# A two-branch gated encoder layer in one kernel: squares over dead tiles, early embedding loads, paired output stores, a later spread of 1/rms

## The chip, the cores and the metric

The kernel runs on one core of a Trainium2 chip. The metric is the device time of one execution in microseconds (us), and the time of a version is the median of its runs. All work is in float32; the products are made of fp32r matmuls on high and low parts, so that one product of 128 x 1024 weights by 1024 x 512 activations is 24 matmuls (8 K tiles, times high by high, high by low and low by high).

## What is computed

One layer on 2048 tokens of width 1024, then a last RMSNorm. Cut to what matters here:

```python
h = _rmsnorm(x, norm_g[i])
proj = jnp.einsum('bsd,dn->bsn', h, w_in[i]) + b_in[i]
u, v, za, ab, ab_gate, zb, g_a, g_b = jnp.split(proj, SPLIT_IDX, axis=-1)
y_a = _spatial_gating_branch(gelu(u), gelu(v), za, ...)      # 128 x 128 position mixer per group
y_b = _conformer_conv_branch(ab, ab_gate, zb, ...)           # causal depthwise conv, 31 taps
merged = sigmoid(g_a) * (y_a @ w_pa[i]) + sigmoid(g_b) * (y_b @ w_pb[i])
x = x + merged @ w_out[i]
ple_gate = sigmoid(_rmsnorm(x, ple_norm_g[i]) @ w_ple_gate[i])
x = x + ple_gate * (p[i] @ w_ple[i])
return _rmsnorm(x, final_g)
```

## The kernel before

**Layout.** Activations lie transposed: 128 channels on the partitions (a K tile), tokens along the row. The tokens are two "sups" of 1024, each of two blocks of T = 512.

**Stages.** `front(sup)` norms x, makes v for 512 tokens and then for the other 512, and runs the 20 units of `ORDER` (u, z, conv and gates, seven products each, `unit`). For sup 0 the products of the per-layer embedding (`st_ple`) stand between the two halves of v; their results go to the DRAM tile `ple`. `part_a_of(sup)` multiplies branch A by w_pa. `back(sup)` multiplies branch B by w_pb (`st_pb`), the merged activations by w_out (`st_out`), and the normed result by w_ple_gate (`st_pgate`), each for block i0 and then block i1; `rms` and `x1_norm` or `finish` of one block stand beside the products of the other. The program is front(0), part_a_of(0), front(1), back(0) and part_a_of(1), back(1). The last stage of back(1) is `st_pgate` of the last block in two halves of 256 tokens (`last`), so that its first half can be finished beside the second.

**Order.** Nothing is issued by hand. `Plan` records every operation with an estimated cost and the tiles it touches, simulates PE, DVE, ACT and one queue of DMAs (SP), and pins the order of each engine to what comes out. Tiles come from rings that are opened in the order of the program (`BUFS`: 7 tiles of 512 columns in "a", 4 of 1024 in "r", 4 of 1024 in "d", 28 of 1024 in "B"). A ring's tile can be opened only when an older one is free. Each engine and the SP queue work strictly in the pinned order. So one operation that opens one tile less moves others that share its ring.

**Helpers.** Each operation is recorded in a helper, and so the profile gives most of them a helper's line: L228 two-tensor operations (`tt`), L231 scalar-tensor-tensor (`stt`), L235 `ts`, L241 ACT (`ac`; L240 a table load ahead of a logarithm), L250 matmuls, L257 DMAs. The names in the profile are rings: `a` is a work tile, `B` an activation tile or a resident weight, `s` a sum, a total of weights or an rms tile, `ps` PSUM, `r` raw weights or x.

**What the change touches.**
- `add_square` squares an updated tile of the residual into a new work tile on ACT, and DVE adds it to `b.ss`. `st_out` calls it after it adds the product to `xt` (x from DRAM), `st_pgate` after it adds the gated embedding `s * p`.
- `rms` sums `b.ss` over channels with one matmul (ps <- s, con) and makes 1/rms on ACT and DVE. For the input's norm `x_rms` does that with tiny tiles, and then spreads the factor over the partitions: four `ts` scale the identity by it into a work tile (a <- con, xs), and one float32 matmul with a matrix of constants (ps <- a, con, two records in the trace) makes `b.rx`, which `x_quarters` multiplies x by.
- `st_pgate` loads `p`, its 512 (or 256) columns of `ple`, into a work tile.
- `finish` scales one K tile of the residual and stores it.

Of the kernel before, what the change touches and what calls it, by code (L numbers as in the profile page):

```python
# [10 lines left out]
ALU = mybir.AluOpType  # L11
PSUM = bass.MemoryType.PSUM

P = 128
S = 2048
D = 1024
# [197 lines left out]
def hybrid_trunk_kernel(  # L214
# [19 lines left out]
    def ts(out, a, s0, s1, op0, op1=ALU.bypass):  # L234
        ins = nc.vector.tensor_scalar(out, a, s0, s1, op0, op1)  # L235
        plan.add("dve", out.free_size() / (0.96 if a.space == PSUM else 1.92) + 140, ins, out, a, s0, s1)
# [18 lines left out]
    def dma(out, a):  # L255
        ns = 4 * P * out.free_size() / DMA_RATE
        plan.add("dma", ns, nc.sync.dma_start(words(out), words(a)), out, a)  # L257
# [7 lines left out]
    def work(dt=F32):  # L265
        return ring("a", [T], dt)

    def slots(n, dt=F32R):

        four = [[ring("B", [2, T], dt) for _ in range(n)] for _ in range(KT // 2)]  # L270
        return [[four[k // 2][i][:, k % 2, :] for k in range(KT)] for i in range(n)]

    def psum(tag="ps", bufs=6):
        return psp.tile([P, T], F32, name=tag, tag=tag, bufs=bufs)
# [191 lines left out]
    def rsqrt_small(v, e, out, tmp):  # L466

        ac(tmp, v, AF.Ln, bias=eps[:, e : e + 1])
        ac(out, tmp, AF.Exp, scale=-0.5)
        tt(tmp, out, out, ALU.mult)  # L470
        stt(tmp, v, (RMS_EPS, LN_EPS)[e], tmp, ALU.add, ALU.mult)
        stt(out, tmp, 3.0, out, ALU.subtract, ALU.mult)
        ts(out, out, -0.5, None, ALU.mult)

    def add_square(acc, src, first, h=ALL):
        if first:
            ac(acc, src, AF.Square)
            return
        sq = work()[:, h]
        ac(sq, src, AF.Square)  # L480
        tt(acc, acc, sq, ALU.add)

# [30 lines left out]
    def x_rms(b, h):  # L513

        c = slice(h * NT, h * NT + NT)
        v, r, tmp = (b.xs[:, i, c] for i in range(3))
        ts(v, v, 1.0 / D, None, ALU.mult)
        rsqrt_small(v, 0, r, tmp)
        if h == 1:
            b.rx = ring("r", [2, T])  # L520
        ps, dg = psum(), work()
        for t in range(NT):
            ts(dg[:, t * P : (t + 1) * P], ident, r[:, t : t + 1], float(D), ALU.mult, ALU.mult)
        mm(ps, o1024, dg, True, True)
        ac(b.rx[:, h, :], ps, AF.Copy)

# [222 lines left out]
    def st_out(b, n, w, h=ALL, first=None):  # L749
        first = n == 0 if first is None else first  # L750
        xt = work()[:, h]
        dma(xt, xT[:, n, b.i * T + h.start : b.i * T + h.stop])
        if first and h.start == 0:
            (b.X,) = slots(1, F32)
            b.xnh, b.xnl = slots(2)
            b.ss, b.r = ring("s", [T]), None
        x1 = b.X[n][:, h]
        tt(x1, product(w, b.mh, b.ml, h), xt, ALU.add)
        add_square(b.ss[:, h], x1, first, h)

    def rms(b, h=ALL):
        if b.r is None:
# [7 lines left out]
        stt(t, b.X[k][:, h], half[:, 0, k : k + 1], b.r[:, h], ALU.mult, ALU.mult)  # L770
        split(b.xnh[k][:, h], b.xnl[k][:, h], t)

    def st_pgate(b, n, w, h=ALL, first=None):
        first = n == 0 if first is None else first
        p = work()[:, h]
        dma(p, ple[:, n, b.i * T + h.start : b.i * T + h.stop])
        s = work()[:, h]
        ac(s, product(w, b.xnh, b.xnl, h), AF.Sigmoid)
        x2 = b.X[n][:, h]
        tt(s, s, p, ALU.mult)  # L780
        tt(x2, x2, s, ALU.add)
        add_square(b.ss[:, h], x2, first, h)

    def finish(b, k, h=ALL):
        o = b.X[k][:, h]
        stt(o, o, half[:, 1, k : k + 1], b.r[:, h], ALU.mult, ALU.mult)
        dma(outT[:, k, b.i * T + h.start : b.i * T + h.stop], o)


    blocks = [Block(i) for i in range(NB)]  # L790
# [3 lines left out]
    def do(f, *a):  # L794
        seq.append((0.0, None, lambda w: f(*a)))

    def std(w, n, f, *a):
        seq.append((5.5, lambda: load_w(w, n), lambda got: f(*a, got)))
# [15 lines left out]
    def ple_of(i, c, w):  # L814
        if w:
            ple_w[c] = w
        st_ple(i, c, ple_w[c])
# [3 lines left out]
    def front(b, first, then):  # L821
        def G(j):
            two(b, 32, j, st_gate)
            two(b, 24, j, st_ab)

        def A(j):
            two(b, 0, j, st_u)
            two(b, 16, j, st_za)

        def zb(j):  # L830
            two(b, 40, j, st_keep, AF.Silu, 40, "zb")

        def ga(j):
            two(b, 48, j, st_keep, AF.Sigmoid, 48, "ga")

        def gb(j):
            two(b, 56, j, st_keep, AF.Sigmoid, 56, "gb")

        square = [(x_square, b, t) for t in range(2 * NT)]
        rms = [(x_rms, b, h) for h in range(2)]  # L840
        quarters = [(x_quarters, b, k) for k in range(4)]
        if first:
            beside = [square[4:6], square[6:], rms[1:], [], square[:2], square[2:4], rms[:1] + [(p_split, 0)], [(p_split, 1)]]
            for j, v in enumerate(v_items(b, 1)):
                if j < 4:
                    do(x_raw, b, j)
                if j == 1:
                    do(load_constants)
                std(*v)
                for e in beside[j]:  # L850
                    do(*e)
            do(load_more_constants)
            for j in range(2 * NB):
                i, c = divmod(j, 2)
                seq.append((5.5, (lambda c=c: load_w(w_ple, c)) if i == 0 else None, lambda got, i=i, c=c: ple_of(i, c, got)))
                if c:
                    do(*quarters[i])
                    if i + 2 < NB:
                        do(p_split, i + 2)
            for j in range(8):  # L860
                seq.append((5.5, lambda j=j: load_w(w_v, j, True), lambda got, j=j: st_v(b, 0, j, got)))
            do(setup_mixer)
        else:
            for j, v in enumerate(v_items(b, 1)):
                std(*v)
                if j >= 4:
                    do(*quarters[j - 4])
            mix(v_items(b, 0), [])
        do(v_rms, b)
        if not first:  # L870
            do(pace, 3)
        for f, j in ORDER:
            if (f, j) == ORDER[-1]:
                do(*then)
            dict(G=G, A=A, z=zb, a=ga, b=gb)[f](j)

    def part_a_of(s, rest):
        both = blocks[2 * s : 2 * s + 2]
        for j in range(KT):
            us = 11.0  # L880
            seq.append((us, lambda j=j: load_w(w_pa, j), lambda got, j=j: [st_pa(i, j, got) for i in both]))
            for r in rest[j * len(rest) // KT : (j + 1) * len(rest) // KT]:
                do(*r)

    def back(s, then):
        i0, i1 = blocks[2 * s], blocks[2 * s + 1]
        for n in range(KT):
            std(w_pb, n, st_pb, i0, n)
            if n == 4:
                do(y_load, i1, "yb")  # L890
        for n in range(KT):
            std(w_pb, n, st_pb, i1, n)
        for n in range(KT):
            std(w_out, n, st_out, i0, n)
        mix([(w_out, n, st_out, i1, n) for n in range(KT)], [(rms, i0)] + [(x1_norm, i0, k) for k in range(KT)])
        mix([(w_pg, n, st_pgate, i0, n) for n in range(KT)], [(rms, i1)] + [(x1_norm, i1, k) for k in range(KT)])
        rest = [(rms, i0)] + [(finish, i0, k) for k in range(KT)]
        if then:
            mix([(w_pg, n, st_pgate, i1, n) for n in range(KT)], rest[:5] + then[:1] + rest[5:] + then[1:])
            return [(rms, i1)] + [(finish, i1, k) for k in range(KT)]  # L900
        held = {}

        def last(n, h):
            def run(w):
                held[n] = w or held[n]
                st_pgate(i1, n, held[n], h)

            return run

        halves = [slice(0, T // 2), slice(T // 2, T)]  # L910
        for n in range(KT):
            seq.append((2.9, lambda n=n: load_w(w_pg, n, stay=n < 6), last(n, halves[0])))
            if n == 1:
                do(rms, i0)
        rest = [(finish, i0, k) for k in range(KT)]
        rest[4:4] = [(rms, i1, halves[0])]
        for n in range(KT):
            seq.append((2.9, None, last(n, halves[1])))
            for r in rest[n * len(rest) // KT : (n + 1) * len(rest) // KT]:
                do(*r)  # L920
        do(rms, i1, halves[1])
        for h in halves:
            for k in range(KT):
                do(finish, i1, k, h)
# [11 lines left out]
    b = sups[1]  # L936
    early = [(x_square, b, t) for t in (4, 5, 6, 7)] + [(x_rms, b, 1)] + [(x_raw, b, k) for k in range(4)]
    do(pace, 1)
    part_a_of(0, early + [(x_square, b, t) for t in range(4)] + [(x_rms, b, 0)])
    do(pace, 2)  # L940
    front(sups[1], False, (y_load, blocks[0], "yb"))
    do(pace, 4)
# [79 lines left out]
```

## Time and profile before

| | us |
|---|---|
| median of 3 runs | 2138.9 (2136.34 to 2139.3) |
| the profiled execution, its own time | 2135.81 |
| its span (first to last instruction) | 2133.9 |
| PE busy (TensorE matmuls) | 2089.7, 98% |
| DVE busy (VectorE) | 1672.6, 78% |
| ACT busy (ScalarE) | 1070.4, 50% |
| mean granted TensorE clock | 0.990 of 2.4 GHz |

The span is what the trace covers; the execution's own time is 1.9 us longer, and the median of the runs another 3.1 us. Busy times are sums over the span. In a timeline, consecutive instructions of one kind are put into one row: start, length from the first to the last one's end, engine, line, operation, and the count, and in brackets the engine's idle time before the row and what ended it. PE rows of one product or many are 24 matmuls or a multiple, unless another kind stands between them.

### The profile page before, as it was taken

To read this page: it belongs to the slowest core of one execution; us is meant where nothing else is said; L and a number is where in the kernel's file an instruction comes from. 1 tells how busy PE (TensorE), PEld (TensorE's weight loads), DVE (VectorE), ACT (ScalarE), POOL (GpSimd) and SP (SyncE) were. 2 spreads that over 40 slices of the span, in tenths; PEclk is the share of its full clock that TensorE was granted. 3 is DMA by queue.
4 is the path that set the end of the run, shared out by engine and by line. 5 is a ranking of instruction groups with operands and counts; after the bars stand their busy time and mean duration, and the time that the engine had idled before them with its cause. 6 is when DMAs were issued, how large, how long until landed. Compare 5 with 4: busy or idle time off the path is not lost.

```text
span 2133.9 us, 26416 instructions
## 1 busy us (share of the span) xinstructions
PE 2089.7 (98%) x9354; PEld 1717.3 (80%) x9354; DVE 1672.6 (78%) x2237; ACT 1070.4 (50%) x1542; POOL 0.2 (0%) x4
## 2 busy tenths in 40 slices
PE   9999999999999999999999999999999999999997
PEld 7878888888888878878878788887888877888877
DVE  4777999999999969878879898889866774464675
ACT  6635464555556733255445555556544551232453
POOL 0000000000000000000000000000000000000000
PEclk9999999999999999999999999999999999999999
DMA  8888878788688877787677687778744466674433
GB/s 292 300 335 324 289 260 319 264 313 309 264 321 319 287 276 251 252 278 261 207 257 227 223 293 242 245 257 270 255 152 139 148 233 204 206 236 134 146 121 109
DMA packets 205156, 523.73 MB, mean 245 GB/s; under 512 B 22368, under 2 KB 43232, under 8 KB 205024
## 3 DMA queue, kind: packets, MB, share of 16 engines
q1 hardware_dynamic: 205024, 522.05, 71.1%
q8 instruction: 73, 1.20, 0.2%
q14 instruction: 59, 0.48, 0.1%
HBM read 326.81 MB, written 195.16 MB: 245 GB/s over the span
## 4 chain that ended last, share of the span: by engine, by line
PE 89%; DMA 4%; DVE 3%; ACT 2%; issue 1%; SPq 0%; DVEq 0%; ACTq 0%
PE ps L250 88%; PE pq L250 1%; DMA r<-w_v 1%; DMA r<-x 1%; DVE d L231 1%; ACT a L241 1%; DMA a<-ple 1%; DVE B L228 1%; DVE a L228 0%; DMA w<-w 0%; DVE w L228 0%; ACT w L241 0%; ACT d L241 0%; DMA r<-V 0%; DVE a L231 0%
## 5 line engine op out<-in xcount | busy, mean ns | idle before, releaser
L250 PE MATMUL ps<-B,w 128*128 128x512 f32 (+1 forms) x7680 | 1773.0, 390 | 13.4 <-ACT B L241 4.5
L250 PEld LDWEIGHTS ps<-B,w 128*128 128x128 f32 x7680 | 1434.8, 188 | 328.2 <-ACT a L241 12.1
L231 DVE SCALAR_TENSOR_TENSOR d<-c,cw,d 128x1024 f32<-128x1024 f32 x464 | 574.2, 1281 | 3.3 <-ACT d L241 2.9
L228 DVE TENSOR_TENSOR w<-r,w 128x1024 fp32r<-128x1024 f32 (+1 forms) x208 | 209.6, 1008 | 158.1 <-PE ps L250 109.2
L241 ACT CAST w<-r 128x1024 fp32r<-128x1024 f32 (+1 forms) x208 | 182.0, 876 | 273.7 <-PE ps L250 226.9
L228 DVE TENSOR_TENSOR a<-ps,a 128x512 f32<-128x512 f32 x176 | 121.3, 689 | 92.8 <-PE ps L250 60.0
L250 PE MATMUL ps<-w,B 128*128 128x512 f32 x768 | 183.1, 399 | 6.2 <-ACT B L241 2.8
L250 PEld LDWEIGHTS ps<-w,B 128*128 128x128 f32 x768 | 146.7, 192 | 42.1 <-ACT w L241 4.3
L241 ACT COPY a<-ps 128x512 f32<-128x512 f32 x88 | 51.0, 590 | 186.4 <-PE ps L250 185.9
L241 ACT ACT_TABLE_LOAD x93 | 119.3, 1283 | 2.3 <-PEq L1013 0.7
L241 ACT CAST B<-a 128x512 fp32r<-128x512 f32 x128 | 76.4, 619 | 70.0 <-DVE a L228 38.7
L228 DVE TENSOR_TENSOR a<-a 128x512 f32<-128x512 f32 (+1 forms) x136 | 86.6, 657 | 30.5 <-ACT a L241 20.9
L241 ACT ACTIVATE a<-ps,bi 128x512 f32<-128x512 f32 x96 | 66.2, 689 | 81.7 <-PE ps L250 81.2
L228 DVE TENSOR_TENSOR B<-a,B 128x512 fp32r<-128x512 f32 x128 | 84.7, 689 | 27.4 <-ACT B L241 27.2
L241 ACT CAST w<-s 128x512 fp32r<-128x512 f32 x112 | 69.0, 618 | 66.2 <-issue 30.0
L228 DVE TENSOR_TENSOR n<-d,n 128x512 fp32r<-128x512 f32 (+1 forms) x96 | 65.9, 688 | 21.4 <-ACT d L241 10.3
L228 DVE TENSOR_TENSOR w<-s,w 128x512 fp32r<-128x512 f32 x112 | 76.6, 688 | 5.6 <-ACT w L241 5.1
L241 ACT ACTIVATE a<-a,bi 128x512 f32<-128x512 f32 x96 | 68.8, 720 | 23.1 <-DVE a L228 22.2
L241 ACT ACTIVATE a<-B 128x512 f32<-128x512 f32 (+1 forms) x63 | 36.8, 584 | 71.3 <-DVE B L228 71.3
L241 ACT ACTIVATE a<-ps 128x512 f32<-128x512 f32 (+1 forms) x96 | 53.4, 557 | 36.0 <-PE ps L250 35.9
L240 ACT ACT_TABLE_LOAD x47 | 60.3, 1283 | 0.8
L241 ACT CAST B<-r 128x512 fp32r<-128x512 f32 (+1 forms) x62 | 39.6, 664 | 37.5 <-DVE r L231 23.5
(79 smaller groups left out, 1169.6 us busy)
## 6 DMA issues: line engine op xcount, KB each, us to landing
w<-w SPq DMA_DIRECT2D x392, 512.0 KB, 4.1
r<-w_s SPq DMA_DIRECT2D x56, 512.0 KB, 5.4
r<-w_pb SPq DMA_DIRECT2D x32, 512.0 KB, 4.3
r<-w_out SPq DMA_DIRECT2D x32, 512.0 KB, 3.5
r<-w_pg SPq DMA_DIRECT2D x32, 512.0 KB, 3.5
a<-xT SPq DMA_DIRECT2D x48, 256.0 KB, 3.9
c<-glu SPq DMA_DIRECT2D x16, 527.0 KB, 5.2
r<-w_v SPq DMA_DIRECT2D x16, 512.0 KB, 5.9
```

Source lines behind the costliest of these rows:

```text
L228: plan.add("dve", out.free_size() / 0.96 + 152, nc.vector.tensor_tensor(out, a, b, op), out, a, b)
L231: ins = nc.vector.scalar_tensor_tensor(out, a, s, b, op0, op1)
L240: load = [nc.scalar.preload_act_table_set("natural_log_exp_and_others")] if both else []
L241: ins = nc.scalar.copy(out, a) if func == AF.Copy and not kw else nc.scalar.activation(out, a, func, **kw)
L250: plan.add("pe", ns, pe.matmul(out, lhsT=lhsT, rhs=rhs, start=start, stop=stop, **kw), out, lhsT, rhs)
```

## The change

1. `add_square` gets the tile to write the square over: `xt` in `st_out`, `s` in `st_pgate`. It opens no work tile.
2. In the last block's `st_pgate`, `p` of two K tiles and all 512 columns is one DMA of 512 KB into a tile of ring "d", and serves both halves: 4 DMAs in the place of 16 of 128 KB. The `rms` of block i0 is traced after the third half product and not after the second.
3. `finish` stores at every second K tile, two K tiles in one DMA: 20 stores in the place of 40.
4. The spread of 1/rms is a function of its own, `x_spread`, and is traced later than `x_rms`.

```diff
+    class Tiles(list):
+        pass
+
     def slots(n, dt=F32R):
 
         four = [[ring("B", [2, T], dt) for _ in range(n)] for _ in range(KT // 2)]
-        return [[four[k // 2][i][:, k % 2, :] for k in range(KT)] for i in range(n)]
+        out = []
+        for i in range(n):
+            out.append(Tiles(four[k // 2][i][:, k % 2, :] for k in range(KT)))
+            out[i].tiles = [f[i] for f in four]
+        return out
...
-    def add_square(acc, src, first, h=ALL):
+    def add_square(acc, src, first, sq):
         if first:
             ac(acc, src, AF.Square)
             return
-        sq = work()[:, h]
         ac(sq, src, AF.Square)
         tt(acc, acc, sq, ALU.add)
...
         rsqrt_small(v, 0, r, tmp)
+
+    def x_spread(b, h):
+
         if h == 1:
             b.rx = ring("r", [2, T])
         ps, dg = psum(), work()
         for t in range(NT):
-            ts(dg[:, t * P : (t + 1) * P], ident, r[:, t : t + 1], float(D), ALU.mult, ALU.mult)
+            r = b.xs[:, 1, h * NT + t : h * NT + t + 1]
+            ts(dg[:, t * P : (t + 1) * P], ident, r, float(D), ALU.mult, ALU.mult)
...
-        add_square(b.ss[:, h], x1, first, h)
+        add_square(b.ss[:, h], x1, first, xt)
...
-    def st_pgate(b, n, w, h=ALL, first=None):
-        first = n == 0 if first is None else first
-        p = work()[:, h]
-        dma(p, ple[:, n, b.i * T + h.start : b.i * T + h.stop])
+    def st_pgate(b, n, w, h=ALL, p=None):
+        first = n == 0
+        if p is None:
+            p = work()
+            dma(p, ple[:, n, b.tok])
...
-        add_square(b.ss[:, h], x2, first, h)
+        add_square(b.ss[:, h], x2, first, s)
...
-        dma(outT[:, k, b.i * T + h.start : b.i * T + h.stop], o)
+        if k % 2:
+            dma(outT[:, k - 1 : k + 1, b.i * T + h.start : b.i * T + h.stop], b.X.tiles[k // 2][:, :, h])
...
-            beside = [square[4:6], square[6:], rms[1:], [], square[:2], square[2:4], rms[:1] + [(p_split, 0)], [(p_split, 1)]]
+            beside = [square[4:6], square[6:], rms[1:], [], square[:2] + spread[1:], square[2:4], rms[:1] + [(p_split, 0)], [(p_split, 1)]]
...
+                if j == 0:
+                    do(*spread[0])
...
             for j, v in enumerate(v_items(b, 1)):
                 std(*v)
+                if j == 0:
+                    do(*spread[0])
...
-                st_pgate(i1, n, held[n], h)
+                if n % 2 == 0 and w:
+                    held["p"] = ring("d", [2, T])
+                    dma(held["p"], ple[:, n : n + 2, i1.tok])
+                p = held.setdefault((n, "p"), held["p"][:, n % 2, :])
+                st_pgate(i1, n, held[n], h, p[:, h])
...
-            if n == 1:
+            if n == 2:
                 do(rms, i0)
...
-    part_a_of(0, early + [(x_square, b, t) for t in range(4)] + [(x_rms, b, 0)])
+    part_a_of(0, early + [(x_square, b, t) for t in range(4)] + [(x_rms, b, 0), (x_spread, b, 1)])
```

Where the planner puts things differs in four places only: the first 60 us, the end of part_a_of(0) with the start of front(1), the end of back(0), and back(1). Three of them follow.

On PE at the start of the program: `ps<-w,B` are v products (sup 0, the second 512 tokens), `ps<-d,w` the products of the embedding, `ps<-a,con` the two spreads.

```order
-L250 MATMUL ps<-w,B 128x512 x73
-L250 MATMUL ps<-a,con 128x512
-L250 MATMUL ps<-w,B 128x512 x111
-L250 MATMUL ps<-a,con 128x512
-L250 MATMUL ps<-w,B 128x512 x8
-L250 MATMUL ps<-d,w 128x512 x192
+L250 MATMUL ps<-w,B 128x512 x132
+L250 MATMUL ps<-a,con 128x512
+L250 MATMUL ps<-w,B 128x512 x60
+L250 MATMUL ps<-d,w 128x512 x24
+L250 MATMUL ps<-a,con 128x512
+L250 MATMUL ps<-d,w 128x512 x168
```

Both spreads moved back, the second of them from 8 matmuls ahead of the embedding's products to 24 matmuls into them. In front(1) they moved too: before, the first stood 240 matmuls ahead of the end of part_a_of(0) and the second at that end; now the first stands at that end, and the second one v product (24 matmuls) later.

On the SP queue at the end of back(0), before (`ya_117` is branch A's result in DRAM, `outT` the output, `ple` the embedding's products, `w_pa` weights of the next stage):

```order
L257 DMA r<-w_pa 128x1024
L257 DMA outT<-B 128x512 x3
L257 DMA a<-ya_117 128x512 x8
L257 DMA a<-ple 128x512
L257 DMA r<-w_pa 128x1024 x3
L257 DMA a<-ple 128x512
L257 DMA a<-ya_117 128x512 x8
L257 DMA a<-ple 128x512
```

The same place in the changed kernel:

```order
L257 DMA r<-w_pa 128x1024
L257 DMA outT<-B 128x2x512
L257 DMA a<-ya_117 128x512 x6
L257 DMA outT<-B 128x2x512
L257 DMA a<-ya_117 128x512 x2
L257 DMA a<-ple 128x512 x2
L257 DMA r<-w_pa 128x1024 x2
L257 DMA a<-ya_117 128x512 x4
L257 DMA outT<-B 128x2x512
L257 DMA a<-ya_117 128x512 x4
L257 DMA a<-ple 128x512
```

Two `a<-ple` moved ahead of the weights of the next stage, and between the two groups of eight `a<-ya_117` stand two loads of weights and not three.

On the SP queue through the last two stages of back(1) (`w_pg` weights of `st_pgate`), before:

```order
L257 DMA r<-w_pg 128x1024 x2
L257 DMA a<-ple 128x512
L257 DMA r<-w_pg 128x1024
L257 DMA a<-ple 128x512
L257 DMA r<-w_pg 128x1024
L257 DMA a<-ple 128x256 x4
L257 DMA outT<-B 128x512
L257 DMA a<-ple 128x256
L257 DMA outT<-B 128x512 x5
L257 DMA a<-ple 128x256
L257 DMA outT<-B 128x512 x2
L257 DMA a<-ple 128x256 x9
```

And in the changed kernel, to the end of the queue:

```order
L257 DMA r<-w_pg 128x1024
L257 DMA a<-ple 128x512
L257 DMA r<-w_pg 128x1024
L257 DMA a<-ple 128x512
L257 DMA r<-w_pg 128x1024 x2
L257 DMA a<-ple 128x512
L257 DMA r<-w_pg 128x1024
L257 DMA outT<-B 128x2x512 x4
L257 DMA outT<-B 128x2x256 x8
```

The loads of 256 columns are gone from here (the four loads in their place stand earlier, among the weights of the w_pb stage of back(1)), and only output stores are left behind the last weights.

## Rows read from the trace of the kernel before

**Rows 1.** The page: busy time, share of the span and instructions of each engine.

```profile
PE 2089.7 (98%) x9354; PEld 1717.3 (80%) x9354; DVE 1672.6 (78%) x2237; ACT 1070.4 (50%) x1542; POOL 0.2 (0%) x4
```

**Rows 2.** Waits of PE over the whole span: us in total, times, longest.

```profile
PE ps L250 <- ACT B L241: 10.5, 4, 4.5
PE ps L250 <- DVE s L228: 7.8, 3, 4.6
```

**Rows 3.** Windows: length, busy us (instructions) of the engines, PEclk, DMA share, GB/s.

```profile
750.00:775.00 25.00, 22.83 (x92) 18.11 (x91) 16.18 (x23) 11.51 (x17) 0.00 (x0) 0.93 0.89 311
1750.00:1775.00 25.00, 19.13 (x69) 14.33 (x68) 16.76 (x25) 11.19 (x18) 0.00 (x0) 0.86 0.77 257
2050.00:2100.00 50.00, 44.96 (x292) 41.09 (x290) 38.54 (x64) 24.59 (x42) 0.00 (x0) 0.93 0.40 136
```

**Rows 4.** Timeline of PE, then DVE, at the start of front(1).

```profile
753.48 1.13 PE L250 MATMUL ps<-a,con 128*128 128x512 f32 x2 [2.17 <-DVE a L235]
...
810.92 87.62 PE L250 MATMUL ps<-w,B 128*128 128x512 f32 x384
...
867.58 0.68 DVE L228 TENSOR_TENSOR B<-r,B 128x512 fp32r<-128x512 f32 x1
```

**Rows 5.** Timeline of SP, DVE, ACT and PE at the end of back(0).

```profile
1741.30 8.05 SPq L257 DMA_DIRECT2D r<-w_pa  x3
...
1749.91 7.19 SPq L257 DMA_DIRECT2D a<-ya  x8
...
1753.29 0.69 DVE L228 TENSOR_TENSOR a<-a 128x512 f32<-128x512 f32 x1 [2.25 <-DMA a<-ple]
...
1754.80 0.63 ACT L241 ACTIVATE a<-B 128x512 f32<-128x512 f32 x1 [4.00 <-DVE B L228]
...
1755.99 8.50 PE L250 MATMUL ps<-B,w 128*128 128x512 f32 x24 [4.46 <-ACT B L241]
1765.87 1.13 PE L250 MATMUL ps<-s,con 128*128 128x512 f32 x2 [1.38 <-DVE s L228]
```

**Rows 6.** Timeline of SP, ACT and PE as the last stage of back(1) begins.

```profile
2057.91 2.07 SPq L257 DMA_DIRECT2D r<-w_pg  x2
2060.03 0.43 SPq L257 DMA_DIRECT2D a<-ple  x1
...
2066.95 0.63 ACT L241 ACTIVATE a<-B 128x512 f32<-128x512 f32 x1 [4.92 <-DVE B L228]
...
2068.63 4.87 PE L250 MATMUL ps<-B 128*128 128x256 f32 x24 [3.23 <-ACT B L241]
2075.26 1.86 PE L250 MATMUL ps<-s,con 128*128 128x512 f32 x2 [1.76 <-DVE s L228]
```

**Rows 7.** Timeline of ACT, DVE and PE in the last 16 us.

```profile
2119.11 0.37 ACT L241 ACTIVATE a<-ps 128x256 f32<-128x256 f32 x1
...
2121.14 0.42 DVE L228 TENSOR_TENSOR a<-a 128x256 f32<-128x256 f32 x1
...
2123.32 1.22 PE L250 MATMUL ps<-s,con 128*128 128x256 f32 x2 [4.63 <-DVE s L228]
...
2127.26 3.26 DVE L231 SCALAR_TENSOR_TENSOR B<-B,half,s 128x256 f32<-128x256 f32 x8
```

**Rows 8.** Timeline of DVE, SP and ACT as the embedding's products begin.

```profile
53.50 0.88 DVE L235 TENSOR_SCALAR a<-con,xs 128x128 f32<-128x128 f32 x4
...
60.03 1.39 SPq L257 DMA_DIRECT2D V<-a  x3
...
66.55 1.09 ACT L241 COPY a<-ps 128x512 f32<-128x512 f32 x2 [0.40 <-DMA V<-a]
```

**Rows 9.** DMA issues: count, KB each, median us from issue to landing.

```profile
V<-a SPq DMA_DIRECT2D x32, 256.0 KB, 3.8
...
outT<-B SPq DMA_DIRECT2D x24, 256.0 KB, 3.2
...
outT<-B SPq DMA_DIRECT2D x16, 128.0 KB, 1.8
```

More of the change, by code (lines that the diff above doesn't have):

```diff
@@ L839, in front @@
         square = [(x_square, b, t) for t in range(2 * NT)]
-        rms = [(x_rms, b, h) for h in range(2)]
+        rms, spread = ([(f, b, h) for h in range(2)] for f in (x_rms, x_spread))
         quarters = [(x_quarters, b, k) for k in range(4)]
         if first:
-            beside = [square[4:6], square[6:], rms[1:], [], square[:2], square[2:4], rms[:1] + [(p_split, 0)], [(p_split, 1)]]
+            beside = [square[4:6], square[6:], rms[1:], [], square[:2] + spread[1:], square[2:4], rms[:1] + [(p_split, 0)], [(p_split, 1)]]
             for j, v in enumerate(v_items(b, 1)):
```

## The prediction

> **What bounds the kernel now.** I read the page's busy times first: TensorE works for 2089.7 of 2133.9 us, 98% [rows 1]. So nothing that runs beside it counts, and what can be won is in its gaps and in the stretches at half clock. Next PE's waits by releaser: the two largest entries are a cast on ACT (ACT B, four gaps, 10.5 us) and the sum of squares on DVE (DVE s, three gaps, 7.8 us) [rows 2]. Then the windows around these gaps, which give idle time and clock together [rows 3]: a 25 us window loses 25 less PE's busy time, and (1 − clock) x 25 more. In 750 to 775 us that is 2.17 + 1.75 = 3.9 us; in 1750 to 1775, 5.87 + 3.5 = 9.4; in the 50 us from 2050, 5.04 + 3.5 = 8.5. Last the timelines of the engines at these places [rows 4 to 8], to see what each gap waits for. The change moves work in just these places and at the start.
>
> **Second front (751 us).** Before, the first spread's matmul stands between products of part_a, and PE waits 2.17 us for its four scalings on DVE [rows 4]. Now it stands behind all of them, 240 matmuls later; a matmul takes 87.62/384 = 0.228 us [rows 4], so DVE has some 55 us more. The second spread stands one product (24 x 0.228 = 5.5 us) later than it did, which starts the four quarters of x later; their last DVE step was at 867.58 and they are needed when the v products end, at 810.92 + 87.62 = 898.5 [rows 4]. Those 30 us of slack hide it. I take the whole loss, **−3.9**; with the gap alone and no clock it is −2.2.
>
> **End of back(0) (1751 us).** SP stands in three loads of w_pa for 8.05 us [rows 5], and one `a<-ple` and eight `a<-ya` queue behind them. DVE then idles 2.25 us for that `a<-ple`; its add releases the square, which ACT waited 4.00 us for; behind the square in ACT's order are the casts of branch A's tiles, and PE, at 1755.99, has waited 4.46 us for one of them. DVE is then late with the sum of squares too: another 1.38 us of PE [rows 5]. Now two `a<-ple` go ahead of the weights, eight `a<-ya` ahead of both, and the square opens no tile of ring "a", so loads into it are let go sooner. The casts can pass ACT before the late squares. What is late next would be the last eight `a<-ya`, behind two w_pa loads in place of three: by 8.05 x 2/3 = 5.4 us of SP they are 2.7 us sooner, and the last `a<-ple` is no longer ahead of them. I take nearly all of the 9.4: **−9.3**; the gaps alone (4.46 + 1.38) are −5.8.
>
> **Last stage (2065 us).** Again `a<-ple` is issued behind two loads (w_pg, 2.07 us of SP), ACT waits 4.92 us for the add and PE 3.23 us for the cast behind the square, then 1.76 us for the sum of squares [rows 6]. Now a load of w_pg and one of ple alternate, no loads of half tiles crowd ring "a", and `rms` comes one half product later. PE has two half products of 24 matmuls to work on ahead of it and not one; 24 took 4.87 us at the lower clock [rows 6] and would take about 2.9 at the full one (an estimate: 4.87 with 1.75 to 2 us of clock loss taken off). The sum must follow its product by an eviction, two adds, a square and an add, so I leave 0.6 us of waiting: 8.5 − 0.6 = **−7.9**; the gaps alone are −5.0, and nothing left to wait −8.5.
>
> **Tail.** After the last product PE idles 4.63 us for the sum [rows 7]. In it the gate is evicted by 2119.48, but DVE takes it at 2121.14, since scalings of the first half stand ahead of it. With `rms` of the first half one product sooner in DVE's new order, most of these 1.66 us go; I take 1.3. Against that, the last stores are of 256 KB: a store of that size lands in 3.2 us, one of 128 KB in 1.8 [rows 9], so +1.4, less one issue at the end, which takes 1.39/3 = 0.46 us [rows 8]. Together −1.3 + 1.4 − 0.5 = **−0.4**, between −2.0 (landing no longer, and all 1.66) and +0.9 (DVE no sooner).
> The Trainium skill, "DMA: Bandwidth & Descriptors", Anatomy of one DMA, gives each transfer a fixed part and bytes at 436 GB/s; by that 128 KB more cost 0.3 us, an estimate, and the tail would be −1.5. Its fit is of another way of issuing; the sum here goes by the rows.
>
> **Start.** Here the change adds a wait. The second spread's four scalings took 0.88 us and were in time [rows 8]; now its matmul stands 24 matmuls into the embedding's products, and its work tile comes free only when a store of v has landed. Three such stores are issued from 60.03 us, a store takes 3.8 us by its median [rows 9], and ACT, waiting for one of them, went on only at 66.55 [rows 8], 6.5 us after. So the scalings start between 63.8 and 66.5 and end 0.9 us later, while PE is there at about 63 (the embedding's products began at some 58, and 24 matmuls are 5.5). PE waits 1.7 to 4.4 us, in order, with all later products queued behind it, and may lose 1.75 us of clock as it did after the gap at 753 [rows 3]. I take 2.2 + 1.75, less 0.6 for small waits for the embedding's inputs, which are now loaded sooner: **+3.3**. The ends are −0.6 (the store lands in time) and +6.7 (4.4 + 1.75, and 0.6 at the first spread, which is now 59 matmuls later). The quarters start later here as well; as above, what they feed is far off.
>
> Squares over dead tiles and early ple loads cost nothing themselves: the same squares, and four loads of 512 KB in a stage where the DMA engines are busy 0.40 of the time or so [rows 3].
>
> **Sum:** −3.9 − 9.3 − 7.9 − 0.4 + 3.3 = −18.2, against the profiled execution's 2135.8: 2117.6. The runs' median stands 3.1 above that execution, so **2120.7** for the median. The ends: −3.9 − 9.4 − 8.5 − 2.0 − 0.6 = −24.4 (2114.5), and with gaps alone −2.2 − 5.8 − 5.0 + 0.9 + 6.7 = −5.4 (2133.5).
>
> **The rivals.**
> *Start clean.* The store lands in time and the early wait is −0.6: 2120.7 − 3.9 = 2116.8. The median of 3.8 speaks for it, the 6.5 of just that place against.
> *The stall at 1751 comes back.* Two loads of w_pa still hold SP ahead of the last `a<-ya`, and if the casts of the second eight wait as long as the first did, 9.3 us are not won: 2130.0.
> *The clock stays.* Behind each gap the rows show a half-clock stretch [rows 3], and I took them for its effect. If they are not, 1.75 + 3.5 + 3.5 us stay and the start loses none: 2120.7 + 8.75 − 1.75 = 2127.7. [...]
> *No change.* With PE at 98%, each wait just moves to the next late cast: 2138.9. The slack in rows 4 speaks against it.
> *Slower.* A tile that holds x or the gate now lives on through the square and the sum. If the seven tiles of ring "a" then come free later, the next product's eviction waits for a tile, PSUM stays full and PE waits: at the DVE wait of 2.25 us [rows 5] in each of the 16 products of the two `st_pgate` stages that stand beside loads of other tiles, 36 us, 2156.7. It makes the kernel slower from (18.2 + 4.3)/16 = 1.4 us in each. Against it: a product opens two tiles now and not three, and lasts 5.5 us, so a tile would have to live for some 19 us.
>
> **How the numbers follow.** A measurement of this kernel tells 0.2%, 4.3 us, from no change. Forecast 0.55, start clean 0.12, stall back 0.14, clock 0.06: all faster, 0.87. No change 0.07. Slower 0.06. The range takes in the four faster cases and most of the bounds: 2113 to 2132.
>
> **What would show it.** Right: no PE wait on DVE a near 751, none over 1 us on ACT B near 1751 and 2065, clock 1.00 in these windows, a new wait of 1 to 4 us for DVE a near 63 us, and about 3.3 us for the last sum. Wrong: `a<-ya` casts still late behind w_pa, or a gap of PE in front(1) ahead of its first unit. The rest of the trace should be as before, shifted.

## The result, and the profile after

The changed kernel takes 2114.64 us (median of 4 runs, 2111.93 to 2115.85), the kernel before 2137.62 in the same runs (2133.91 to 2139.3). The ratio is 0.990, 95% interval 0.9881 to 0.9918. That is 23.0 us less, where 18.2 were forecast; the forecast time was 2120.7 with a range of 2113 to 2132. The profiled execution took 2111.93 us, its span is 2109.3 and its mean granted clock 0.995. Ratios are of the fast runs alone: two executions beside the experiments, of 4254.91 and 8261.13 us, are left out of them.

The page's span and busy times:

```profile
span 2109.3 us, 26318 instructions
...
PE 2077.8 (99%) x9354; PEld 1709.7 (81%) x9354; DVE 1670.5 (79%) x2237; ACT 1071.1 (51%) x1542; POOL 0.2 (0%) x4
```

PE's busy time fell by 11.9 us, from 2089.7 to 2077.8 [rows 1], with the same 9354 matmuls. Nearly all of that is clock: the granted mean rose from 0.990 to 0.995, some 11 us over the span (an estimate). The other half of the span's 24.6 us, 12.7 us, is gaps.

PE's waits by releaser (us in total, times, longest):

```profile
PE ps L250 <- ACT w L241: 4.0, 2, 3.3
PE ps L250 <- DMA w<-w: 4.0, 2, 2.3
PE ps L250 <- DVE s L228: 3.8, 2, 2.6
...
PE ps L250 <- ACT B L241: 1.9, 1, 1.9
PE ps L250 <- DVE a L235: 1.5, 1, 1.5
```

ACT B went from 10.5 us to 1.9, and that one wait is in the first 8 us; DVE s from 7.8 to 3.8 [rows 2]. The wait for the spread's scalings, DVE a L235, is still there, but at another place (61 us). What leads now, casts of w_v and loads of kept weights, was there before, with 2.8 and 4.3 us.

The windows that answer to [rows 3]: length, busy us (instructions) of PE, PEld, DVE, ACT and POOL, PEclk, DMA share, GB/s. The places have moved up by 0 to 21 us.

```profile
740.00:765.00 25.00, 24.34 (x108) 19.80 (x107) 21.74 (x30) 17.89 (x26) 0.00 (x0) 1.00 0.85 300
1745.00:1770.00 25.00, 23.79 (x103) 19.03 (x102) 19.09 (x27) 10.72 (x15) 0.00 (x0) 1.00 0.89 307
2045.00:2095.00 50.00, 50.00 (x393) 48.65 (x392) 37.34 (x72) 26.29 (x50) 0.00 (x0) 1.00 0.25 88
```

Clock 1.00 in all three, against 0.93, 0.86 and 0.93; idle 0.7, 1.2 and 0 us, against 2.2, 5.9 and 5.0.

To see where the time goes, I compare when PE reaches the same work in the two profiles. In the kernel before (timeline of PE: start, length, operation, idle time ahead and its releaser), besides the row of the sum at 1765.87 [rows 5] and that of the last sum at 2123.32 [rows 7]:

```profile
743.39 0.40 PE L250 MATMUL pq<-n,conr 128*128 128x512 f32 x1
...
898.37 6.96 PE L250 MATMUL ps<-B,w 128*128 128x512 f32 x30
...
1200.69 5.53 PE L250 MATMUL ps<-B,w 128*128 128x512 f32 x16 [2.26 <-DMA w<-w]
...
2112.77 5.92 PE L250 MATMUL ps<-B,w 128*128 128x256 f32 x48
```

In the changed kernel:

```profile
743.40 0.40 PE L250 MATMUL pq<-n,conr 128*128 128x512 f32 x1
...
894.49 5.83 PE L250 MATMUL ps<-B,w 128*128 128x512 f32 x25
...
1195.21 10.97 PE L250 MATMUL ps<-B,w 128*128 128x512 f32 x40 [2.32 <-DMA w<-w]
...
1753.20 1.12 PE L250 MATMUL ps<-s,con 128*128 128x512 f32 x2 [1.21 <-DVE s L228]
...
2091.30 5.92 PE L250 MATMUL ps<-B,w 128*128 128x256 f32 x48
2099.79 0.75 PE L250 MATMUL ps<-s,con 128*128 128x256 f32 x2 [2.57 <-DVE s L228]
```

| from, to | forecast | what PE gained there |
|---|---|---|
| start to the conv's matmul at 743 us | +3.3 | 743.40 − 743.39 = 0.0 |
| to the first unit of front(1) | −3.9 | 894.49 − 898.37 = −3.9 |
| to a wait for kept weights near 1200 us | 0 | −5.5, so −1.6 |
| to the sum of squares at the end of back(0) | −9.3 | 1753.20 − 1765.87 = −12.7, so −7.2 |
| to the last two products | −7.9 | 2091.30 − 2112.77 = −21.5, so −8.8 |
| to the end | −0.4 | spans 2109.3 − 2133.9 = −24.6, so −3.1 |
| sum | −18.2 | −24.6 |

The three large terms came about, one to the tenth, one 2.1 us smaller and one 0.9 us larger than forecast. The rest of the difference is in the start, in a stretch that the change does not touch, and in the tail.

SP at the end of back(0), against [rows 5]:

```profile
1733.90 2.30 SPq L257 DMA_DIRECT2D r<-w_pa  x2
1736.30 2.21 SPq L257 DMA_DIRECT2D a<-ya  x4
...
1740.04 4.52 SPq L257 DMA_DIRECT2D a<-ya  x4
```

The last eight `a<-ya` are issued from 1736.30 in two groups, and not from 1749.91. SP still stands 2.3 us in w_pa loads, but no longer 8.05.

### The profile page after: what moved, and what is told of

It is laid out like the page before. It is cut to its first block, busy times and chain, and to the rows that moved or that the text cites. A ratio compares the mean times of both kernels' runs of the same rounds, so it can differ in the third digit from the quotient of the medians.

```text
span 2109.3 us, 26318 instructions
## 1 busy us (share of the span) xinstructions
PE 2077.8 (99%) x9354; PEld 1709.7 (81%) x9354; DVE 1670.5 (79%) x2237; ACT 1071.1 (51%) x1542; POOL 0.2 (0%) x4
## 4 chain that ended last, share of the span: by engine, by line
PE 90%; DMA 5%; DVE 3%; ACT 2%; issue 1%; SPq 0%; DVEq 0%; ACTq 0%
PE ps L250 88%; PE pq L250 1%; DMA a<-ya 1%; DMA r<-w_v 1%; DVE d L231 1%; ACT a L241 1%; DMA r<-w_ple 0%; DVE w L228 0%; DVE B L228 0%; DMA w<-w 0%; ACT w L241 0%; ACT d L241 0%; DVE a L228 0%; DMA r<-V 0%; SPq L257 0%
## 5 line engine op out<-in xcount | busy, mean ns | idle before, releaser
L228 DVE TENSOR_TENSOR a<-a 128x512 f32<-128x512 f32 x120 | 79.7, 685 | 9.8 <-ACT a L241 8.7
L228 DVE TENSOR_TENSOR s<-s,a 128x512 f32<-128x512 f32 (+1 forms) x63 | 39.6, 629 | 27.0 <-ACT a L241 26.8
```

The lines of the kernel that those rows point to most:

```text
L228: plan.add("dve", out.free_size() / 0.96 + 152, nc.vector.tensor_tensor(out, a, b, op), out, a, b)
```

## The experiments

Two theories were set against each other for the large terms. Theory one: a square in a work tile of its own takes one of seven slots of ring "a", and with it the order in which loads are let go. Theory two: the 32 DMAs fewer (12 embedding loads and 20 stores; the first expectation counts 36) relieve the SP queue. Ratios are to the kernel before in runs made beside each experiment; the changed kernel's own is 0.990 (0.9881 to 0.9918).

**Squares in ring a again.**

```diff
-        ac(sq, src, AF.Square)
+        sq = work()[:, : src.free_size()]
+        ac(sq, src, AF.Square)
```

> The changed kernel with squares written into a new work tile again; all else as changed. Theory one (a square's tile costs a slot of the seven in ring a, and so sets the order in which the SP queue lets loads go): the order of the end of back(0) and of the last w_pg loads goes most of the way back, PE waits some 3 to 4.5 us for a cast near 1750 us and 2 to 3 us as the last stage begins, each with half clock behind it: +9 to +14 us, 2124 to 2129. Theory two (early loads of ple and paired stores, 36 DMAs fewer, relieve the SP queue): those stay, so within 2 us of the changed kernel, about 2115.

Measured: 2127.59 us, ratio 0.9972 (0.9959 to 0.9985). Its timeline of PE at the two places, and of SP at the first:

```profile
1757.63 8.93 PE L250 MATMUL ps<-B,w 128*128 128x512 f32 x24 [4.71 <-ACT B L241]
1767.95 1.13 PE L250 MATMUL ps<-s,con 128*128 128x512 f32 x2 [1.38 <-DVE s L228]
...
2071.09 6.22 PE L250 MATMUL ps<-B 128*128 128x256 f32 x36 [2.16 <-ACT B L241]
...
1750.30 0.33 SPq L257 DMA_DIRECT2D r<-w_pa  x1
1750.73 0.37 SPq L257 DMA_DIRECT2D a<-ple  x1
1751.20 7.55 SPq L257 DMA_DIRECT2D a<-ya  x8
```

The waits of before are back (4.71 and 1.38 us where 4.46 and 1.38 stood, and 2.16 in the last stage where 3.23 stood), and the last eight `a<-ya` are issued from 1751.20, as late as before. All other parts of the change were in this kernel. Theory two is out as the cause of these waits. By the medians this kernel is still 7.0 us faster than the one before: no wait stands near 751 us, the sum in the last stage waits 0.41 us in place of 1.76, and the last sum 3.43 in place of 4.63.

**Squares in ring n.** Is it the slot in "a", or the shorter chain when a tile is overwritten?

```diff
-        ac(sq, src, AF.Square)
+        sq = ring("n", [T])[:, : src.free_size()]
+        ac(sq, src, AF.Square)
```

> The changed kernel with squares in a tile of their own again, but of ring n, which is free in these stages, and not of ring a. Theory one (only the slot in ring a counts): the gains at 1750 us and in the last stage stay, PE's waits there below 1.3 us, within 3 us of the changed kernel: 2112 to 2116. Rival (writing over the dead tile itself brings the gain, by a shorter chain from add to square to sum): back to the kernel with squares in ring a, 2125 to 2130.

Measured: 2116.07 us, ratio 0.9912 (0.9893 to 0.9932). PE, then SP, at the end of back(0):

```profile
1734.71 20.79 PE L250 MATMUL ps<-B,w 128*128 128x512 f32 x91
1757.10 1.12 PE L250 MATMUL ps<-s,con 128*128 128x512 f32 x2 [1.60 <-DVE s L228]
...
1737.99 5.47 SPq L257 DMA_DIRECT2D a<-ya  x7
```

No wait for a cast, 1.60 us for the sum, which is a little over the 1.3 expected, and none in the last stage; seven of the last eight `a<-ya` are issued from 1737.99, early as in the changed kernel. The square may have a tile of its own, but not one of this ring: it is the slot.

**Squares over dead tiles alone**, on the kernel before:

```diff
-    def add_square(acc, src, first, h=ALL):
+    def add_square(acc, src, first, sq):
...
-        sq = work()[:, h]
...
-        add_square(b.ss[:, h], x1, first, h)
+        add_square(b.ss[:, h], x1, first, xt)
...
-        add_square(b.ss[:, h], x2, first, h)
+        add_square(b.ss[:, h], x2, first, s)
```

> The kernel before with the first part of the change alone: squares over the dead tiles. Theory: this part alone takes the gap near 1750 us down to 0.5 to 1.5 us and that at the last stage's beginning down as well, where the second sum (rms of block 2 after the second half product) still waits 1.5 to 2.5 us; the gap of 2.2 us at 751 us stays. Against the kernel before -10 to -14 us, 2121 to 2126. Rival: it needs the early loads of ple too, so that ring a is free in the last stage; then the last stage keeps its waits of 3.2 and 1.8 us and only some 7 us are won, 2128 to 2130.

Measured: 2121.29 us against 2133.06, ratio 0.9942 (0.9926 to 0.9957): −11.8 us of medians, about half of the whole gain. Its timeline of PE:

```profile
751.15 1.12 PE L250 MATMUL ps<-a,con 128*128 128x512 f32 x2 [2.17 <-DVE a L235]
...
1739.67 18.07 PE L250 MATMUL ps<-B,w 128*128 128x512 f32 x79
1757.97 1.13 PE L250 MATMUL ps<-s,con 128*128 128x512 f32 x2 [0.23 <-DVE s L228]
...
2062.77 1.13 PE L250 MATMUL ps<-s,con 128*128 128x512 f32 x2 [2.39 <-DVE s L228]
```

At the end of back(0) 0.23 us are left; in the last stage only the wait for the second sum, 2.39; the wait of 2.17 us at 751 us stays, as it should. This kernel has as many loads and stores as the one before, so the waits for the casts go without fewer DMAs. The wait ahead of the last sum goes down too, to 2.63 us from 4.63.

**The last block's embedding loaded late again** (16 DMAs of 128 KB into ring "a"):

```diff
-                if n % 2 == 0 and w:
-                    held["p"] = ring("d", [2, T])
-                    dma(held["p"], ple[:, n : n + 2, i1.tok])
-                p = held.setdefault((n, "p"), held["p"][:, n % 2, :])
-                st_pgate(i1, n, held[n], h, p[:, h])
+                p = work()[:, h]
+                dma(p, ple[:, n, i1.i * T + h.start : i1.i * T + h.stop])
+                st_pgate(i1, n, held[n], h, p)
```

> The changed kernel with the last block's ple loaded per half and per K tile again (16 DMAs of 128 KB into ring a). Theory one: the last stage still begins without a wait, because loads of ple for block 2 still alternate with w_pg; the end loses 0 to 2 us by adds that wait for late ple tiles: 2115 to 2117. Theory two: the wait as the last stage begins comes back with its clock, +5 to +8: 2120 to 2123.

Measured: 2114.33 us, ratio 0.9906 (0.9886 to 0.9926): its interval covers no difference from the changed kernel. Its trace has no wait of PE over 0.4 us in the last stage, and 2.63 us ahead of the last sum (2.57 with the early loads). With the squares out of ring "a", the loads of half tiles crowd nothing.

**The sum one half product sooner:**

```diff
-            if n == 2:
+            if n == 1:
                 do(rms, i0)
```

> The changed kernel with rms of block 2 traced after the second half product again. Theory: the sum of squares is not ready when PE comes to it one half product (2.9 us) sooner: a wait of 0.5 to 3 us for DVE s near 2055 us, +0.5 to +4.5 with clock: 2115 to 2119. Rival: the loads come so much sooner that the sum is ready anyway: no wait, 2114 to 2115.

Measured: 2116.45 us, ratio 0.9919 (0.9898 to 0.994). PE in the last stage:

```profile
2065.17 2.07 PE L250 MATMUL ps<-s,con 128*128 128x512 f32 x2 [2.39 <-DVE s L228]
```

The wait comes back, 2.39 us, and the two records of the sum take 2.07 us where the same two take 1.13 at full clock (in the kernel with squares over dead tiles alone): half clock stands behind it in this profile (granted clock 0.76 from 2062 to 2068 us). The median of the runs is only 1.8 us above that of the changed kernel and its interval covers no difference, so the wait is shown and its price is not. Of the last stage's gain it is a part that the squares do not bring.

**Single stores again:**

```diff
-        if k % 2:
-            dma(outT[:, k - 1 : k + 1, b.i * T + h.start : b.i * T + h.stop], b.X.tiles[k // 2][:, :, h])
+        dma(outT[:, k, b.i * T + h.start : b.i * T + h.stop], o)
```

> The changed kernel with one store for each K tile again (40 stores). By the landing times of the rows (256 KB 3.2 us, 128 KB 1.8) the end after the last scaling would be 1.4 us shorter less 0.5 for the issues: -0.9. Rival (what ends the kernel is the number of issues and the fixed part of a transfer): the same or up to 1 us longer. At 1750 us PE's waits as in the changed kernel. In all 2113 to 2117.

Measured: 2118.14 us, ratio 0.9919 (0.9901 to 0.9937), 1 us above what was expected, and not told apart from the changed kernel by its interval. In its profile the last scaling ends at 2114.28 and the span at 2118.0, 3.7 us later; in the changed kernel these are 2106.17 and 2109.3, 3.1 us. In the other two profiles with single stores, the kernel before and the one with squares over dead tiles alone, it is 3.4 and 3.3 us. So pairing shortens the very end by 0.2 to 0.6 us; the forecast had it 0.9 longer.

**The second front's spreads, back at the sums.**

```diff
-    part_a_of(0, early + [(x_square, b, t) for t in range(4)] + [(x_rms, b, 0), (x_spread, b, 1)])
+    part_a_of(0, early + [(x_square, b, t) for t in range(4)] + [(x_rms, b, 0), (x_spread, b, 0)])
...
-    early = [(x_square, b, t) for t in (4, 5, 6, 7)] + [(x_rms, b, 1)] + [(x_raw, b, k) for k in range(4)]
+    early = [(x_square, b, t) for t in (4, 5, 6, 7)] + [(x_rms, b, 1), (x_spread, b, 1)] + [(x_raw, b, k) for k in range(4)]
...
                 std(*v)
-                if j == 0:
-                    do(*spread[0])
```

> The changed kernel with the second front's two spreads traced where they were before (directly behind their sums of squares). If the wait of 2.17 us at 751 us and its half clock were the spread's place alone: +3 to +4 us, 2118 to 2118.5, all of it between 740 and 760 us. If that time had only moved to the waits at 742, 913 and 1393 us that the changed kernel has: no difference, 2114 to 2115.

Measured: 2109.9 us, ratio 0.9896 (0.9875 to 0.9917): not slower. But its DVE and PE near 751 us show that this was not a true undo:

```profile
744.50 0.87 DVE L235 TENSOR_SCALAR a<-con,xs 128x128 f32<-128x128 f32 x4
...
751.03 1.02 PE L250 MATMUL ps<-a,con 128*128 128x512 f32 x2
```

The first spread stands on PE where it stood before, with no wait, because DVE's four scalings are done by 745.4. Two more items beside part_a's products than before had shifted the planner's order on DVE. So I undid it exactly, with the spread inside `x_rms` for the second sup:

```diff
         rsqrt_small(v, 0, r, tmp)
+        if b.s:
+            x_spread(b, h)
...
-    part_a_of(0, early + [(x_square, b, t) for t in range(4)] + [(x_rms, b, 0), (x_spread, b, 1)])
+    part_a_of(0, early + [(x_square, b, t) for t in range(4)] + [(x_rms, b, 0)])
...
                 std(*v)
-                if j == 0:
-                    do(*spread[0])
```

> The changed kernel with the second front's spreads inside x_rms again, so that part_a_of(0) has the same 14 items beside its products as before (the earlier undo had 16, which shifted them); on PE and DVE the order around 751 us is that of the kernel before. Theory: the gap of about 2 us for DVE a returns at 751 us, with or without 1.7 us of half clock behind it: +2 to +4 in the stretch 740 to 765 us. Rival (the gap was never the spread's place, but DVE being late for other reasons): no gap there, as in the earlier undo.

Measured: 2118.7 us, ratio 0.9921 (0.9903 to 0.9939). DVE and PE:

```profile
754.07 0.67 DVE L235 TENSOR_SCALAR a<-con,xs 128x128 f32<-128x128 f32 x3
...
754.79 2.00 PE L250 MATMUL ps<-a,con 128*128 128x512 f32 x2 [2.17 <-DVE a L235]
```

The gap of 2.17 us is back to the hundredth, and the two records take 2.00 us where they took 1.02 above: half clock again (granted clock 0.86 from 750 to 762 us). The median is 4.1 us above that of the changed kernel, but the intervals overlap: the gap is shown by the profile, its price in the runs is not. Tracing the spread later is enough to be rid of it, but not needed: the matmul may stay if the scalings do not stand behind the conv's taps on DVE.

**The first front's spreads, back at the sums:**

```diff
-            beside = [square[4:6], square[6:], rms[1:], [], square[:2] + spread[1:], square[2:4], rms[:1] + [(p_split, 0)], [(p_split, 1)]]
+            beside = [square[4:6], square[6:], rms[1:] + spread[1:], [], square[:2], square[2:4], rms[:1] + spread[:1] + [(p_split, 0)], [(p_split, 1)]]
...
-                if j == 0:
-                    do(*spread[0])
                 if c:
```

> The changed kernel with the first front's two spreads traced where they were before. Theory: the wait of 1.3 to 2.4 us for DVE a near 61 us, which all profiles of the late spread show, goes, and 0.6 us of small waits for inputs of the embedding's products come back: -0.7 to -1.8 us, 2112.5 to 2115. Rival: the later stores of v and loads of p cost as much: the same or 1 us slower, up to 2117.

Measured: 2116.16 us, ratio 0.9923 (0.9908 to 0.9937). No wait near 61 us, but 2.8 us near 28 and 1.4 near 56 us, ahead of the spreads' matmuls at their old places: no gain, as the rival had it.

**Only the second of them moved back:**

```diff
-            beside = [square[4:6], square[6:], rms[1:], [], square[:2] + spread[1:], square[2:4], rms[:1] + [(p_split, 0)], [(p_split, 1)]]
+            beside = [square[4:6], square[6:], rms[1:], [], square[:2] + spread[1:], square[2:4], rms[:1] + spread[:1] + [(p_split, 0)], [(p_split, 1)]]
...
-                if j == 0:
-                    do(*spread[0])
                 if c:
```

> The changed kernel with only the second spread of the first front moved back to its sum of squares; the first stays at its late place. Theory: the wait near 61 us goes while the inputs of the embedding's products are still loaded early: -1.3 to -2.4 us, 2112 to 2114. Rival: the time comes back at the waits for casts of w_v near 113 to 126 us: no difference, 2114 to 2117.

Measured: 2112.91 us, ratio 0.9906 (0.9887 to 0.9924). The wait is 0.69 us; the interval covers no difference.

**rx in ring d for the first sup**, to free ring "r" for the weights of v:

```diff
         if h == 1:
-            b.rx = ring("r", [2, T])
+            b.rx = ring("r" if b.s else "d", [2, T])
```

> The changed kernel with the first sup's rx (the spread 1/rms) in ring d and not in r, a version that could beat both. Theory: PE's waits near 112 and 118 us for casts of w_v (0.7 and 3.3 us, and half clock behind) come from ring r, where rx holds one of four tiles while x quarters hold two; with it gone w_v is loaded sooner: -4 to -7 us, 2107.5 to 2110.5. Rival: the loads of w_v are late because the SP queue has the stores of ple ahead of them, which PE's own pace sets: no difference, 2114 to 2115.

Measured: 2116.32 us, ratio 0.9921 (0.9898 to 0.9945). PE in the first front:

```profile
65.42 1.80 PE L250 MATMUL ps<-a,con 128*128 128x512 f32 x2 [3.66 <-DVE a L235]
...
123.94 3.24 PE L250 MATMUL ps<-w,B 128*128 128x512 f32 x12 [0.75 <-ACT w L241]
127.90 19.35 PE L250 MATMUL ps<-w,B 128*128 128x512 f32 x84 [0.72 <-DVE w L228]
...
156.72 3.61 PE L250 MATMUL ps<-B,w 128*128 128x512 f32 x10 [2.25 <-DVE a L228]
```

Ring "r" was indeed what held the casts of w_v: two waits of 0.75 and 0.72 us are left of them, where the changed kernel has 0.7 and 3.3. But the late spread now waits 3.66 us in place of 1.47, and the first unit 2.25 for an eviction of v on DVE, a wait that was not there. The time moved.

**Both together:**

```diff
-            beside = [square[4:6], square[6:], rms[1:], [], square[:2] + spread[1:], square[2:4], rms[:1] + [(p_split, 0)], [(p_split, 1)]]
+            beside = [square[4:6], square[6:], rms[1:], [], square[:2] + spread[1:], square[2:4], rms[:1] + spread[:1] + [(p_split, 0)], [(p_split, 1)]]
...
-                if j == 0:
-                    do(*spread[0])
                 if c:
...
-            b.rx = ring("r", [2, T])
+            b.rx = ring("r" if b.s else "d", [2, T])
```

> The kernel sp0b with the first sup's rx in ring d, a version meant to beat both. Theory: with rx in ring d the waits for casts of w_v near 113 to 126 us were 1.5 us in place of 4 to 5, but the wait for the late spread was 3.7 us; with the spread early that one goes, and the wait of 2.25 us for DVE a near 155 us is left: -3 to -5 us against the changed kernel, 2110 to 2113. Rival: the waits move to the next place again: 2114 to 2117.

Measured: 2109.05 us (2104.33 to 2114.59), ratio 0.9890 (0.9872 to 0.9908). PE in the first front:

```profile
121.29 19.35 PE L250 MATMUL ps<-w,B 128*128 128x512 f32 x84 [0.46 <-DVE w L228]
...
149.77 10.50 PE L250 MATMUL ps<-B,w 128*128 128x512 f32 x38 [1.92 <-DVE a L228]
```

Now the spread costs no wait, the casts of w_v 0.46 us, and the eviction 1.92. Its median is the lowest of all, yet its interval overlaps that of the changed kernel: by the ratios perhaps some 2 us better, not shown.

## Why the prediction was right, and where it was off

**Bound and method.** Right: PE is bound by nothing but its own gaps and clock. The gaps at the spread, at the casts and at the last stage's sum went; those for the sum at the end of back(0), 1.38 us, and for the last sum, 4.63, are still there with 1.21 and 2.57. The time lies 1.6 us above the low end of the range, near the sum of all better ends (2114.5): besides the forecast mechanism it took the luck named below.

**Second front.** Size right, −3.9, in part by luck: some 1.7 us of it is half clock, which the kernel with squares over dead tiles alone does not have behind the same gap (last section). The reason (DVE gets time) holds, by the exact undo; that the spread had to move for it does not, by the first one.

**End of back(0).** Mechanism right: loads into ring "a" are let go sooner once squares do not open it. Mis-sized: −7.2, not −9.3. The sum of squares is still late by 1.21 us, and small new waits of 0.4 us stand ahead of the place. And part of the clock was counted twice, as this window of the kernel before shows:

```profile
1750.00:1756.00 6.00, 1.54 (x8) 0.95 (x6) 2.62 (x4) 2.00 (x5) 0.00 (x0) 0.89 0.97 327
```

Of the 3.5 us, 0.7 (0.11 of 6 us) fell into the gap itself, where PE had no work to lose. The rival "the stall comes back" did not happen; it happens when the square takes a slot again.

**Last stage.** −8.8 for −7.9. I left 0.6 us of waiting and there was none. The four early loads cost PE nothing, but not for the reason given: they run in a stage where the DMA engines are busy 0.76 of the time (1800 to 1850 us) and not 0.40, and PE is busy there without a gap. One reason given falls: the half-tile loads do not crowd the ring (late loads measure the same). The one that carries is the square's slot for the first wait, and the later sum for the second.

**Start.** This step failed: +3.3 forecast, 0.0 measured. It took the issue time of v's stores, 60.03 [rows 8], from the kernel before. SP, DVE and PE in the changed kernel:

```profile
54.81 1.89 SPq L257 DMA_DIRECT2D V<-a  x4
...
60.21 0.87 DVE L235 TENSOR_SCALAR a<-con,xs 128x128 f32<-128x128 f32 x4 [0.42 <-DMA V<-a]
...
61.13 1.12 PE L250 MATMUL ps<-a,con 128*128 128x512 f32 x2 [1.47 <-DVE a L235]
```

The stores are issued from 54.81, since two loads of p that stood among them on SP are gone from there; the scalings begin at 60.21. PE is there at 59.66, and not at about 63, and waits 1.47 us, without half clock behind it (granted clock 1.00 from 50 to 75 us). In the nine profiles with this late spread and rx in ring "r" or "d", the wait is 1.31 to 3.66 us, three times with half clock behind it, so the wait itself was well placed. But the first 170 us also vary by themselves: PE ends its first 60 matmuls of units at 167.0 us in the changed kernel's profile, and at 167.5 to 171.9 in others that have the same order there; with the order of before it is 168.6 us, and 165.9 in the kernel with squares over dead tiles alone. One profile is not enough to size a term of 3 us there, and whether the later spreads cost time at the start stays open.

**Tail.** −3.1 for −0.4. ACT, DVE, and the stores of the last half in the changed kernel:

```profile
2097.25 0.38 ACT L241 ACTIVATE a<-ps 128x256 f32<-128x256 f32 x1 [0.52 <-PE ps L250]
...
2097.67 0.43 DVE L228 TENSOR_TENSOR a<-a,d 128x256 f32<-128x256 f32 x1 [0.26 <-ACT a L241]
...
2102.91 3.26 DVE L231 SCALAR_TENSOR_TENSOR B<-B,half,s 128x256 f32<-128x256 f32 x8
...
outT<-B SPq DMA_DIRECT2D x8, 256.0 KB, 2.1
```

DVE takes the gate at 2097.67, as it is evicted (2097.63), and not 1.66 us after as before; the wait for the last sum is 2.57 in place of 4.63 us. That was forecast with 1.3, and 2.1 came. It comes mostly with the squares: 2.63 us are left with them alone, and 3.43 where only they are undone. Another 0.8 us were won between the start of the last sum's matmul and the end of the last scaling (7.2 us before, 6.4 now), 0.5 of it in the matmul itself (1.22 and 0.75 us), and 0.2 behind that scaling. The sign of the stores was wrong: I priced a 256 KB store at 3.2 us by a median [rows 9] of stores of which two thirds run near 1750 us, where the DMA engines are busy 0.77 of the time [rows 3]; at the end it lands in 2.1, 0.3 more than one of 128 KB. By this the Trainium skill's rule for one transfer ("DMA: Bandwidth & Descriptors", Anatomy of one DMA) was the better price: its 0.3 us, an estimate by its rate, is what the runs show here.

**Clock.** I took a half-clock stretch as the effect of each gap. It is more loosely tied. The rival "the clock stays" is out, for the clock is 1.00 wherever the gap went. But the last section shows gaps without it, and −1.6 us near 1072 is just that: 2.01 us of wait with half clock behind it before, 1.67 without it after. No part of the change stands there, and the kernel with the first front's spreads undone has 2.00 us there without it; so this gain is luck. PE in the kernel before, then in the changed one:

```profile
1074.11 6.23 PE L250 MATMUL ps<-B,w 128*128 128x512 f32 x19 [2.01 <-DMA w<-w]
...
1070.23 10.04 PE L250 MATMUL ps<-B,w 128*128 128x512 f32 x43 [1.67 <-DMA w<-w]
```

The 19 matmuls take 0.33 us each before, the 43 take 0.23 after.

## What to carry to other kernels

Where a planner or a pool lets loads go as ring slots come free, count the tiles that each step opens, not only its instructions: one scratch tile less in a ring of seven was worth some 12 of 23 us put in alone (15 by the ratios when taken out alone), with the same arithmetic, and it did not matter whether the scratch went over a dead tile or into another ring. An undo in such a program has to give the old order back (look at it on each engine), or it tests another program. And take a transfer's price from a place that is as busy as the one where it will run.

## What the runs showed of the hardware

The same gap of 2.17 us at the spread's matmul near 751 us has half clock behind it in one run and not in another. The window 750 to 762 us of the kernel before (clock 0.86):

```profile
750.00:762.00 12.00, 9.83 (x35) 7.33 (x34) 9.40 (x15) 4.54 (x7) 0.00 (x0) 0.86 0.85 299
```

The same window of the kernel with squares over dead tiles alone (clock 1.00, and 11 matmuls more in it):

```profile
750.00:762.00 12.00, 10.85 (x46) 8.65 (x47) 9.25 (x14) 6.14 (x9) 0.00 (x0) 1.00 0.88 309
```

Over the 13 profiles of changed kernels, no gap of under 1.7 us inside the program stands directly ahead of a half-clock stretch that I could put down to it, while gaps of 2.2 to 2.3 us near 1195 us have one in six of eight, and none in that of the first undo of the second front's spreads (2.29 us) or of both changes together (2.21 us). In the kernel with squares in ring "n" even 3.06 us there has none. So a gap of some 2 us may cost 1.7 us more (0.14 of 12 us in the first window) or not, which by an estimate from the several such gaps of each profile moves a run of this kernel by several us. What decides it, the runs do not show. The Trainium skill ("TensorE: Matmul & The Clock Gate", HAM oscillation) ties the lower clock to long idle stretches between bursts; by that none of these gaps should have brought it. The traces agree for the gaps of under 1.7 us, and not for the six of eight near 1195 us.
